# A recurrent scan's small products placed differently: output products behind the next chunk's solved rows, triangular products of eight chunks in one run

## The chip, the cores and the metric

The kernel runs on one core of a Trainium2 chip. Its five engines work side by side, each through its own list of instructions in order: TensorE (PE, matrix products into PSUM), VectorE (DVE), ScalarE (ACT), GpSimd (POOL) and SyncE (SP), which issues the transfers. The metric is the device time of one execution in microseconds; lower is better.

## What is computed

A decoder trunk of two layers on 1024 tokens of width 1024. Each layer normalizes its input, projects it (`h @ w_in`), runs three token mixers (pooling, retention, RWKV-7), gates and projects each, merges them and adds the result to the residual. The change concerns RWKV-7 alone, 8 heads of width 64:

```python
def step(S, inp):
    r_t, w_t, k_t, v_t, a_t, b_t = inp
    sa = jnp.einsum('bhvk,bhk->bhv', S, a_t)
    S = (S * w_t[:, :, None, :] + sa[..., None] * b_t[:, :, None, :]
         + v_t[..., None] * k_t[:, :, None, :])
    return S, jnp.einsum('bhvk,bhk->bhv', S, r_t)

_, y = lax.scan(step, jnp.zeros((B, H, N, N), jnp.float32), xs)
```

Everything else of the layer (`proj = h @ w_in`, the branch and output projections) is large matrix products.

## The kernel before

**Work.** The large products run as 128 x 128 weights against 128 x 512 moving columns; each value is split into a high and a low part, so that three products stand for one (`hhi`, `hlo` against `wh`, `wl`). The RWKV recurrence is computed in chunks of 64 tokens: 16 chunks for 1024 tokens, two heads at a time, so four head pairs (`hp`) in each of two layers make eight scans. `rwkv_task` is the generator for one head pair:

- `prepare(h)` makes, for each half `h` of eight chunks, the tiles `AR` (receptance and key side) and `BK` (key and value side).
- `scores(h)` transposes `BK` into `BKt`, then multiplies `BK` by `AR` for each chunk and head. The result is masked by VectorE into the triangular matrices `G`. Each head's operands stand on 64 partitions, so the products of two heads use 64 rows of the array each. This is done in two groups of four chunks, `q` = 0 and 1, each group written to two banks of PSUM, `gps`, and each followed by two masked multiplies.
- `invert`, `states` and `blocks` solve the triangular systems of all chunks ahead of the scan; `AV` holds what does not depend on the state.
- the scan then goes through the chunks `c` = 0 to 15. For each: the product `sa` of `AR` with the state `S` (into `cy`); VectorE adds `AV` and gives `xst`; two products per head pair give the solved rows (into `ch`), which ScalarE copies to `Z`; the state product `BKt` by `Z` gives the new state `Sn` on VectorE; and the output products `G` by `Z`, one for each head, are added in `cy` to what `sa` left there, and ScalarE copies them to `y`. After eight chunks `y` is normalized and handed to `rwkv_post`.

All of these are float32 products, and each appears in the profile as two instructions.

**PSUM.** There are eight banks: three for the large products (`acc`), two taken in turn by small work (`mx`), and three in the pool `psc`: the two halves of `two`, which `cyt()` gives out alternately, and `ch`.

**Order.** Nothing runs when it is written. Class `Log` records each operation with its operands; `plan()` lists all operations in an order for each engine by estimated durations, dependencies and a key (the place in the program plus `BIAS` of the lane; the lane `rwkv` goes 3000 places ahead); `emit()` then writes the instructions in this order, fixed at build time. Operations inside `with nc.together()` become one unit that stays in one run. An entry `o.after[p] = 2` says that `o` may be placed once `p` has started, without waiting for its end. While the operations are recorded, generators yield times in nanoseconds that decide when the next part is recorded among the large products. PE gets the large products wherever no operation of a lane with a lower key is ready.

**Exemption in the scan.** `sa` of chunk `c` writes one half of `two` while the copy of the output of chunk `c - 1` reads the other. `sa.no_dep` takes away that dependency, and `sa.own_dep` puts in the one on the copy of chunk `c - 2`, which reads the same half.

All instructions are recorded through one line of `emit()`, so that the profile shows line 550 for all, and its rows are told apart by the names of tiles: `ch<-xst,G` are the solved rows, `ch<-Z,BKt` the state product, `two<-Z,G` the output products, `two<-S,AR` the product `sa`, `g<-AR,BK` and `two<-AR,BK` the triangular products, `av<-Z,G` the products of `states`, and `acc<-...` the large products.

Of the kernel before, what the change touches and what calls it, by code (L numbers as in the profile page):

```python
# [9 lines left out]
F32 = mybir.dt.float32  # L10
# [3 lines left out]
ALU = mybir.AluOpType  # L14
# [3 lines left out]
P = 128  # L18
# [4 lines left out]
HF = 512  # L23
# [7 lines left out]
RWKV_EPS = 64e-5  # L31
# [532 lines left out]
def trunk_kernel(ctx, tc, xT, cvec, pos, vecs, consts, w_ada, w_all, pool_w, lora_w, out):  # L564
    nc = Log(tc.nc, tc)
# [15 lines left out]
    ps_c = pool("psc", 1, space=PSUM)  # L581
# [9 lines left out]
    def nm(s):  # L591
        uid[0] += 1
        return f"{s}_{uid[0]}"
# [9 lines left out]
    t_ri = slot("ri", 14)  # L603
# [7 lines left out]
    def mx(s):  # L611
        t = ps_m.tile([P, HF], F32, tag="mx", name=nm(s))
        if len(mxq) == 2:
            behind[t.name] = mxq.popleft()
        mxq.append(t.name)
        return t
# [4 lines left out]
    def cyt():  # L621
        turn[0] ^= 1
        return two[:, turn[0] * HF : (turn[0] + 1) * HF]
# [7 lines left out]
    o = CST["bone"]  # L631
    bone = cp.tile([P, P], F32R, name="bone")
    xst = cp.tile([P, P], F32, name="xst")
# [174 lines left out]
    hd = [dp.tile([8, 2, P, HF], F32, name=f"hd{l}") for l in range(L)]  # L808
# [11 lines left out]
    behind = {}  # L820
# [56 lines left out]
    def wait(*aps, spare=0.0):  # L877
        settle()
        names = [x.tensor.name if hasattr(x, "tensor") else x.name for x in aps]
        t = max(ready.get(n, 0.0) for n in names) + spare  # L880
        if len(mxq) == 2:
            t = max(t, ready.get(mxq[0], 0.0) + 600)
        return max(0.0, t - clock[0])
# [55 lines left out]
    def add(k, task):  # L939
        if not lanes[k]:  # L940
            due[k] = clock[0]
        lanes[k].append(task)
        return task

    def mmul(out, lhsT, rhs, start=True, stop=True, timed=False, **kw):
        n = rhs.free_size()
        fast = rhs.dtype == F32R
        settle()
        await_(out, *(() if timed else (lhsT, rhs)))
        m = lhsT.free_size()  # L950
        clock[0] += (n + 32) / 2.4 if fast else 2 * max(n, 1.6 * m - 92, m - 16) * 0.875
        return nc.tensor.matmul(out, lhsT=lhsT, rhs=rhs, start=start, stop=stop, **kw)
# [10 lines left out]
    posts = {}  # L963
# [236 lines left out]
    def layer_norm(y, n, w, eps, tile_, eng=nc.vector):  # L1200
        y3 = y.rearrange("p (n w) -> p n w", w=w)
        mean = sp.tile([P, n], F32, tag="mn", name=nm("mn"))
        nc.vector.tensor_reduce(mean, y3, axis=mybir.AxisListType.X, op=ALU.add)
        nc.vector.tensor_scalar_mul(mean, mean, 1.0 / w)
        yc = tile_("yc")
        yc3 = yc.rearrange("p (n w) -> p n w", w=w)
        eng.tensor_tensor(
            yc3, y3, mean.unsqueeze(2).to_broadcast([P, n, w]), op=ALU.subtract
        )
        sq = tile_("ysq")  # L1210
        nc.scalar.square(sq, yc)
        var = sp.tile([P, n], F32, tag="vr", name=nm("vr"))
        nc.vector.tensor_reduce(
            var, sq.rearrange("p (n w) -> p n w", w=w), axis=mybir.AxisListType.X, op=ALU.add
        )
        rsqrt(var, eps, 1.0 / w)
        eng.tensor_tensor(yc3, yc3, var.unsqueeze(2).to_broadcast([P, n, w]), op=ALU.mult)
        return yc
# [81 lines left out]
    def rwkv_task(l, hp, kT, rT, vp, lt):  # L1300
        lw = lora_load(l, hp)
        AR = r8("AR").rearrange("p (c j t) -> p c j t", j=2, t=CH)
        BK = r8("BK").rearrange("p (c j t) -> p c j t", j=2, t=CH)
        Gf = gtile("G")
        G = Gf[:, 0 : 32 * P].rearrange("p (u n) -> p u n", n=P)
# [3 lines left out]
        Z = r8("Z").rearrange("p (c n) -> p c n", n=P)  # L1309
        pc = sp.tile([P, 16], F32, tag="pc", name=nm("pc"))  # L1310
        c3 = lambda t: t.rearrange("p (c t) -> p c t", t=CH)
        rm = cs("rmask", P).unsqueeze(1).to_broadcast([P, 4, P])
        jt = lambda t, rows, c: t[rows, c, :, :].rearrange("p j t -> p (j t)")
        bvs, rks = [], []
# [91 lines left out]
        def scores(h):  # L1406
            yield max(until(whole[h] + 1000), wait(Z, spare=600))
            for q in range(2):
                ps = mx("bt")
                c0 = 8 * h + 4 * q  # L1410
                n = min(4, 15 - c0)
                with nc.together():
                    for c in range(n):
                        trans(ps[:, c * P : (c + 1) * P], jt(BK, slice(0, P), c0 + c), timed=True)
                nc.scalar.copy(BKt[:, c0 : c0 + n, :], ps[:, 0 : n * P].rearrange("p (c n) -> p c n", n=P))
                yield 1300
            for q in range(2):
                c0 = 8 * h + 4 * q
                gps = [mx("g"), cyt()]
                with nc.together():  # L1420
                    for j in range(4):
                        for hd in range(2):
                            rows = slice(64 * hd, 64 * hd + 64)
                            mmul(gps[hd][:, j * P : (j + 1) * P], jt(BK, rows, c0 + j), jt(AR, rows, c0 + j), timed=True)
                for hd in range(2):
                    u0 = 16 * hd + c0
                    nc.vector.tensor_tensor(
                        G[:, u0 : u0 + 4, :], gps[hd].rearrange("p (u n) -> p u n", n=P), rm, op=ALU.mult
                    )
                yield 2600  # L1430
            yield from bonus(h)
# [9 lines left out]
        start = [0.0]  # L1441
# [85 lines left out]
        for S in SS:  # L1527
            nc.gpsimd.memset(S, 0.0)
        yield wait(MT, *SS)
        yout = []  # L1530
        for c in range(16):
            par = c % 2
            prog[(l, hp)] = c
            if c % 8 == 0:
                y = t_ri("y")
            S, Sn = SS[par], SS[1 - par]
            cy = cyt()
            if c == 0:
                nc.scalar.copy(xst[0:64, :], AV[:, 0:P])
            else:  # L1540
                if c < 15:
                    SP = sb.tile([P, P], F32, tag="SP", name=nm("SP"), bufs=1)
                    nc.scalar.activation(SP, S, AF.Copy, scale=pc[:, c : c + 1])
                sa = mmul(cy[:, 0:P], jt(AR, slice(0, P), c), S)
                sa.no_dep = yout[-1]
                sa.after[yout[-1]] = 2
                if c > 1:
                    sa.own_dep = yout[-2]
                nc.vector.tensor_tensor(xst[0:64, :], cy[64:128, 0:P], AV[:, c * P : (c + 1) * P], op=ALU.add)
            yield wait(xst)  # L1550
            ch = ps_c.tile([P, HF], F32, tag="ch", name=nm("ch"))
            for hd in range(2):
                cols = slice(64 * hd, 64 * hd + 64)
                u0 = (16 * hd + c) * P
                n = 65
                mmul(ch[0:n, cols], Gf[:, u0 + 64 : u0 + 64 + n], xst[:, cols])
            nc.scalar.copy(Z[0:64, c, :], ch[0:64, 0:P])
            yield wait(Z)
            if c < 15:
                mmul(ch[:, P : 2 * P], BKt[:, c, :], Z[:, c, :])  # L1560
            for hd in range(2 if c < 15 else 0):
                rw = slice(64 * hd, 64 * hd + 64)
                new = ch[rw, P + 64 * hd : P + 64 * hd + 64]
                if c == 0:
                    nc.vector.tensor_scalar_mul(Sn[rw, rw], new, pc[rw, 0:1])
                else:
                    nc.vector.scalar_tensor_tensor(
                        Sn[rw, rw], new, pc[rw, c : c + 1], SP[rw, rw], op0=ALU.mult, op1=ALU.add
                    )
            yield 500  # L1570
            for hd in range(2):
                cols = slice(64 * hd, 64 * hd + 64)
                mmul(
                    cy[0:65, cols],
                    G[:, 16 * hd + c, 0:65],
                    Z[:, c, cols],
                    start=c == 0,
                    skip_group_check=True,
                )
            o = (c % 8) // 2 * P  # L1580
            yout.append(nc.scalar.copy(y[64 * par : 64 * par + 64, o : o + P], cy[0:64, 0:P]).ins)
            yield wait(Sn)
            if c % 8 == 7:
                h = c // 8
                yn = layer_norm(y, 8, 64, RWKV_EPS, t_ri, nc.gpsimd)
                posts[l, hp, h] = add("post", rwkv_post(l, hp, h, yn, bvs[h]))

    def rwkv_post(l, hp, h, yn, bv):
        yield 6500
        yield wait(yn, spare=3000)  # L1590
        ps = mx("yt")
        with nc.together():
            for j in range(4):
                trans(ps[:, j * P : (j + 1) * P], yn[:, j * P : (j + 1) * P])
        ob = t_ri("wob")
        nc.vector.scalar_tensor_tensor(ob, ps, vv(l, "ln_w", hp), bv, op0=ALU.mult, op1=ALU.add)
        store(od[l][2, hp, h], ob)
        yield 100
# [981 lines left out]
```

## Time and profile before

| | |
|---|---|
| three runs, median | 2252.29 us |
| three runs, lowest to highest | 2251.56 to 2252.78 us |
| the profiled run | 2251.25 us |
| its span, first to last instruction | 2249.4 us |
| mean granted clock of TensorE | 0.996 |

The page gives for each engine its busy time. In views by tile or in the timeline a row has the engine, the operation, `out<-in` by the names of tiles, the shapes (for a product: rows x columns of the weights, written 128*65, then the moving operand, 128x64) and a count. Durations of products overlap, since they are pipelined; the distance from one start to the next says what one takes of the engine. A bracket at the end of a row gives the engine's idle time before it and what ended that.

### The profile page before, as it was taken

Reading aid. Unit: us, or ns where it says so; the run is one execution under the profiler, and the core shown is the slowest. Engines: PE = TensorE matmul, PEld = TensorE weight load, DVE = VectorE, ACT = ScalarE, POOL = GpSimd, SP = SyncE. Lnnn points to the kernel's source line nnn. Section 1 sums busy time; section 2 is a strip of 40 time slices with the busy share of each in tenths; the row PEclk is TensorE's granted clock in tenths of the full one; section 3 lists DMA queues with packets and bytes.
Section 4 is the critical chain, followed back from the end, with each engine's and each line's share of the span. In section 5 each row is a group of like instructions: output and inputs, shape, how many; then the busy total and the mean of one; then the engine's idle time right before and its main releaser. Section 6 shows DMA issues by size and latency. Waiting matters only on the chain. (4 is left out here: it accounts for less than half of the span.)

```text
span 2249.4 us, 34694 instructions
## 1 busy us (share of the span) xinstructions
PE 2214.6 (98%) x12836; PEld 1847.6 (82%) x12836; DVE 1637.2 (73%) x2865; ACT 953.6 (42%) x1829; POOL 595.3 (26%) x538
## 2 busy tenths in 40 slices
PE   7999999999999999999999999999999999999998
PEld 6788888888888888888878888888888888888887
DVE  7996886967878765669787678577686844465895
ACT  5634434434344344324464353353443444451254
POOL 2223323333325233320042132333333500041100
PEclk9999999999999999999999999999999999999999
DMA  9222111112236663754440111111123533257343
GB/s 321 69 59 72 34 43 42 48 48 70 85 114 214 201 207 127 238 178 146 145 163 28 48 40 44 48 46 49 36 86 94 176 121 112 86 165 232 117 141 113
DMA packets 138041, 247.77 MB, mean 110 GB/s; under 512 B 15632, under 2 KB 19984, under 8 KB 137872
## 3 DMA queue, kind: packets, MB, share of 16 engines
q1 hardware_dynamic: 137872, 245.56, 34.0%
q8 instruction: 101, 1.65, 0.3%
q14 instruction: 68, 0.56, 0.1%
HBM read 185.99 MB, written 59.51 MB: 109 GB/s over the span
## 5 line engine op out<-in xcount | busy, mean ns | idle before, releaser
L550 PE MATMUL acc<-hhi,wh 128*128 128x512 f32 x1488 | 596.9, 401 | 1.6 <-DVE vp L550 1.1
L550 PE MATMUL acc<-hhi,wl 128*128 128x512 f32 x1488 | 596.8, 401 | 0.0
L550 PE MATMUL acc<-hlo,wh 128*128 128x512 f32 x1488 | 596.4, 401 | 0.0
L550 PEld LDWEIGHTS acc<-hhi,wh 128*128 128x128 f32 x1488 | 280.5, 189 | 50.7 <-DVE vp L550 1.5
L550 PEld LDWEIGHTS acc<-hhi,wl 128*128 128x128 f32 x1488 | 280.6, 189 | 48.6
L550 PEld LDWEIGHTS acc<-hlo,wh 128*128 128x128 f32 x1488 | 280.6, 189 | 47.4
L550 POOL TENSOR_TENSOR wl<-wr,wh 128x512 fp32r<-128x512 f32 x143 | 189.8, 1327 | 474.9 <-ACT wh L550 343.2
L550 ACT CAST wh<-wr 128x512 fp32r<-128x512 f32 x226 | 139.5, 617 | 251.1 <-PE acc L550 191.3
L550 PE MATMUL acc<-T,wh 128*128 128x512 f32 x576 | 177.5, 389 | 0.0
L550 DVE SCALAR_TENSOR_TENSOR S<-ch,pc,SP 64x64 f32<-64x64 f32 x224 | 63.3, 283 | 86.9 <-PE ch L550 84.1
L550 PEld LDWEIGHTS acc<-T,wh 128*128 128x128 f32 x576 | 108.1, 188 | 22.4
L550 ACT CAST wh<-wsum 128x512 fp32r<-128x512 f32 x112 | 69.5, 621 | 121.1 <-PE acc L550 117.3
L550 DVE TENSOR_TENSOR wl<-wsum,wh 128x512 fp32r<-128x512 f32 x79 | 56.2, 712 | 79.0 <-ACT wh L550 78.7
L550 PE MATMUL acc<-T,wl 128*128 128x512 f32 x288 | 112.1, 389 | 0.0
L550 ACT COPY Z<-ch 64x128 f32<-64x128 f32 x128 | 33.1, 259 | 132.3 <-PE ch L550 131.7
L550 DVE TENSOR_TENSOR wl<-wraw,wh 128x512 fp32r<-128x512 f32 x60 | 42.0, 699 | 63.2 <-ACT wh L550 63.2
L550 DVE TENSOR_TENSOR tm<-MT,two 64x30 f32<-64x30 f32 (+14 forms) x240 | 76.3, 318 | 11.4 <-ACT two L550 4.6
L550 POOL TENSOR_TENSOR oz<-ol,oz 128x512 fp32r<-128x512 f32 x10 | 14.1, 1405 | 264.6 <-DVE wl L550 179.7
L550 DVE TENSOR_TENSOR two<-two,tm 64x30 f32<-64x30 f32 (+14 forms) x240 | 78.9, 329 | 7.1
L550 ACT CAST wh<-wraw 128x512 fp32r<-128x512 f32 x84 | 52.0, 619 | 70.8 <-PE acc L550 50.1
L550 PE MATMUL acc<-oy,wh 128*128 128x512 f32 x256 | 80.0, 393 | 0.0
L550 PE MATMUL acc<-oG,wh 128*128 128x512 f32 x256 | 78.9, 389 | 0.0
(340 smaller groups left out, 4914.3 us busy)
## 6 DMA issues: line engine op xcount, KB each, us to landing
wr<-in_w_all SPq DMA_DIRECT2D x246, 256.0 KB, 2.7
wraw<-in_w_all SPq DMA_DIRECT2D x112, 256.0 KB, 2.9
gd<-gsg SPq DMA_DIRECT2D x96, 256.0 KB, 2.0
gs<-gd SPq DMA_DIRECT2D x96, 256.0 KB, 3.5
wada<-in_w_ada SPq DMA_DIRECT2D x80, 256.0 KB, 3.1
ol<-od SPq DMA_DIRECT2D x48, 256.0 KB, 3.6
traw<-hd SPq DMA_DIRECT2D x32, 256.0 KB, 2.9
x<-in_xT SPq DMA_DIRECT2D x16, 256.0 KB, 5.1
```

Source lines behind the costliest of these rows:

```text
L550: o.inst = f(*a, **k)
```

## The change

In `scores` the loop over `q` no longer makes products. One run under `together` makes those of all eight chunks of a half, into four banks: one of `mx`, the two halves of `two`, and `ch`. The masked multiplies stay in the loop.

In the scan the output products, their copy, and the end of a half move into a function `outputs(c, cy, behind)`. It is called for chunk `c - 1` in chunk `c`, after the products of the solved rows and the copy to `Z`, and both heads' products are one unit that may be placed as soon as the last product of the solved rows has started. Chunk 15 gets its own call behind the loop. The exemption of `sa` (`no_dep`, `own_dep`) and the pause of 500 before the outputs are gone.

```diff
+            gps = [mx("g"), cyt(), ps_c.tile([P, HF], F32, tag="ch", name=nm("ch")), cyt()]
+            with nc.together():
+                for j in range(8):
+                    for hd in range(2):
+                        rows = slice(64 * hd, 64 * hd + 64)
+                        o = j % 4 * P
+                        mmul(
+                            gps[j // 4 * 2 + hd][:, o : o + P], jt(BK, rows, 8 * h + j), jt(AR, rows, 8 * h + j), timed=True
+                        )
             for q in range(2):
-                c0 = 8 * h + 4 * q
-                gps = [mx("g"), cyt()]
-                with nc.together():
-                    for j in range(4):
-                        for hd in range(2):
-                            rows = slice(64 * hd, 64 * hd + 64)
-                            mmul(gps[hd][:, j * P : (j + 1) * P], jt(BK, rows, c0 + j), jt(AR, rows, c0 + j), timed=True)
                 for hd in range(2):
-                    u0 = 16 * hd + c0
+                    u0 = 16 * hd + 8 * h + 4 * q
                     nc.vector.tensor_tensor(
-                        G[:, u0 : u0 + 4, :], gps[hd].rearrange("p (u n) -> p u n", n=P), rm, op=ALU.mult
+                        G[:, u0 : u0 + 4, :], gps[2 * q + hd].rearrange("p (u n) -> p u n", n=P), rm, op=ALU.mult
                     )
                 yield 2600
...
-        yout = []
+        ys = [None, None]
+
+        def outputs(c, cy, behind=None):
+            if c % 8 == 0:
+                ys[c // 8] = t_ri("y")
+            y = ys[c // 8]
+            with nc.together():
+                for hd in range(2):
+                    cols = slice(64 * hd, 64 * hd + 64)
+                    o = mmul(
+                        cy[0:65, cols],
+                        G[:, 16 * hd + c, 0:65],
+                        Z[:, c, cols],
+                        start=c == 0,
+                        skip_group_check=True,
+                    )
+            if behind is not None:
+                o.after[behind] = 2
+            o = (c % 8) // 2 * P
+            r = slice(64 * (c % 2), 64 * (c % 2) + 64)
+            nc.scalar.copy(y[r, o : o + P], cy[0:64, 0:P])
+            if c % 8 == 7:
+                h = c // 8
+                yn = layer_norm(y, 8, 64, RWKV_EPS, t_ri, nc.gpsimd)
+                posts[l, hp, h] = add("post", rwkv_post(l, hp, h, yn, bvs[h]))
+
+        cy = None
         for c in range(16):
...
-            cy = cyt()
+            before, cy = cy, cyt()
...
-                sa = mmul(cy[:, 0:P], jt(AR, slice(0, P), c), S)
-                sa.no_dep = yout[-1]
-                sa.after[yout[-1]] = 2
-                if c > 1:
-                    sa.own_dep = yout[-2]
+                mmul(cy[:, 0:P], jt(AR, slice(0, P), c), S)
...
-                mmul(ch[0:n, cols], Gf[:, u0 + 64 : u0 + 64 + n], xst[:, cols])
+                last = mmul(ch[0:n, cols], Gf[:, u0 + 64 : u0 + 64 + n], xst[:, cols])
             nc.scalar.copy(Z[0:64, c, :], ch[0:64, 0:P])
+            if c:
+                outputs(c - 1, before, last)
             yield wait(Z)
...
-            yield 500
-            for hd in range(2):
-                cols = slice(64 * hd, 64 * hd + 64)
-                mmul(
-                    cy[0:65, cols],
-                    G[:, 16 * hd + c, 0:65],
-                    Z[:, c, cols],
-                    start=c == 0,
-                    skip_group_check=True,
-                )
-            o = (c % 8) // 2 * P
-            yout.append(nc.scalar.copy(y[64 * par : 64 * par + 64, o : o + P], cy[0:64, 0:P]).ins)
             yield wait(Sn)
-            if c % 8 == 7:
-                h = c // 8
-                yn = layer_norm(y, 8, 64, RWKV_EPS, t_ri, nc.gpsimd)
-                posts[l, hp, h] = add("post", rwkv_post(l, hp, h, yn, bvs[h]))
+        outputs(15, cy)
```

More of the change, by code (lines that the diff above doesn't have):

```diff
@@ L1533, in rwkv_task @@
             prog[(l, hp)] = c
-            if c % 8 == 0:
-                y = t_ri("y")
             S, Sn = SS[par], SS[1 - par]
-            cy = cyt()
+            before, cy = cy, cyt()
             if c == 0:
```

## The prediction

> **What bounds the kernel now.** I read first the head of the page and the busy time in two windows, then the timeline of TensorE (PE) around single small products, and last the rows of the tiles that the change touches. The head of the page, then the windows (columns: PE, weight loads, VectorE, ScalarE, GpSimd, clock, DMA):
>
> ```profile
> span 2249.4 us, 34694 instructions
> ## 1 busy us (share of the span) xinstructions
> PE 2214.6 (98%) x12836; PEld 1847.6 (82%) x12836; DVE 1637.2 (73%) x2865; ACT 953.6 (42%) x1829; POOL 595.3 (26%) x538
> ```
>
> ```profile
> 0.00:100.00 100.00, 82.01 (x356) 67.04 (x357) 83.65 (x151) 60.52 (x98) 27.83 (x39) 0.95 0.61 217
> 100.00:2249.40 2149.40, 2132.60 (x12482) 1780.55 (x12480) 1553.52 (x2715) 893.09 (x1733) 567.50 (x500) 1.00 0.33 105
> ```
>
> PE is busy for 98% of the span. It stands still for 18.0 us in the first 100 us, which the change does not touch, and for 2149.4 - 2132.6 = 16.8 us in all the rest, at full clock. So after the start there is almost nothing to win by shortening a wait of the scan, and nearly every nanosecond that a step takes away from PE's own stream comes off the time. The question is therefore not how long the chain of a chunk is, but how much PE time its small products take among the large ones. One chunk of the scan, on PE and then on ScalarE (start, duration, instruction):
>
> ```profile
> 187.37 0.40 PE L550 MATMUL acc<-hhi,wl 128*128 128x512 f32 x1
> 187.60 0.40 PE L550 MATMUL ch<-xst,G 128*65 128x64 f32 x4
> 187.81 0.48 PE L550 MATMUL acc<-hhi,wh 128*128 128x512 f32 x1
> 188.13 0.39 PE L550 MATMUL acc<-hlo,wh 128*128 128x512 f32 x1
> ...
> 188.59 0.39 PE L550 MATMUL acc<-hhi,wh 128*128 128x512 f32 x1
> 188.82 0.38 PE L550 MATMUL ch<-Z,BKt 128*128 128x128 f32 x2
> 189.04 0.40 PE L550 MATMUL two<-Z,G 128*65 128x64 f32 x4
> 189.25 0.48 PE L550 MATMUL acc<-hlo,wh 128*128 128x512 f32 x1
> 189.56 0.39 PE L550 MATMUL acc<-hhi,wl 128*128 128x512 f32 x1
> 189.79 0.40 PE L550 MATMUL acc<-hhi,wh 128*128 128x512 f32 x1
> 190.03 0.39 PE L550 MATMUL acc<-hlo,wh 128*128 128x512 f32 x1
> 190.25 0.38 PE L550 MATMUL two<-S,AR 128*128 128x128 f32 x2
> 190.39 0.48 PE L550 MATMUL acc<-hhi,wl 128*128 128x512 f32 x1
> 190.71 0.39 PE L550 MATMUL acc<-hhi,wh 128*128 128x512 f32 x1
> ```
>
> ```profile
> 188.04 0.26 ACT L550 COPY Z<-ch 64x128 f32<-64x128 f32 x1 [1.52 <-PE ch L550]
> 188.20 0.62 ACT L550 CAST wh<-wr 128x512 fp32r<-128x512 f32 x1
> 189.47 0.26 ACT L550 COPY y<-two 64x128 f32<-64x128 f32 x1 [0.65 <-PE two L550]
> ```
>
> Durations overlap, so I price a run of small products by starts. Large products alone follow each other every 0.23 us (189.56, 189.79, 190.03). The price of a run is the time from the large product before it to the second large product after it, less two such steps (0.46). The solved rows alone: 188.13 - 187.37 - 0.46 = **0.30 us**. State product and output products in one run: 189.56 - 188.59 - 0.46 = **0.51 us**. Within a run each instruction of 64 columns costs little, as a long run of the same shape (65 columns of weights, 64 moving) shows:
>
> ```profile
> 279.93 0.48 PE L550 MATMUL acc<-hlo,wh 128*128 128x512 f32 x1
> 280.25 3.00 PE L550 MATMUL av<-Z,G 128*65 128x64 f32 x48
> 283.06 0.48 PE L550 MATMUL acc<-hhi,wl 128*128 128x512 f32 x1
> 283.37 0.40 PE L550 MATMUL acc<-hhi,wh 128*128 128x512 f32 x1
> ```
>
> The 48 cost 283.37 - 279.93 - 0.46 = 2.98 us and the four above 0.30, so one costs (2.98 - 0.30) / 44 = 0.061 us, and a run has 0.30 - 4 x 0.061 = about 0.06 us that is paid once, by the switch from and to large products. That once-paid part is what both halves of the change save.
>
> **The change part by part.** *Outputs behind the solved rows.* Today a chunk pays two such runs with 64-column products: the solved rows, and state plus outputs. Afterwards the outputs of the chunk before stand in the run of the solved rows, and the state product stands alone. No product is added or removed. The new run is not in this trace. From the slope it costs 0.30 + 4 x 0.061 = 0.54 us. Its bounds are 0.51 (187.60 to 187.81 is 0.21 for four, added to 0.30) and 0.60 (two runs of 0.30 that share nothing); I take 0.54, since the 48-product row has the very same shape. The state product alone (two instructions, 128 x 128) is not in the trace either. The nearest row is the S product (two instructions of the same shape) at 190.25. It costs 190.71 - 190.03 - 0.46 = 0.22 us. A chunk then pays 0.54 + 0.22 = 0.76 instead of 0.30 + 0.51 = 0.81: **0.05 us less**, with bounds of 0.08 less and 0.01 more. This applies to 15 chunks in each of 8 scans, 120 in all. The row of the output products, with their first and last start:
>
> ```profile
> L550 PE MATMUL two<-Z,G x512: 217/222/223, 175.7 to 1766.5; 128*65 128x64 f32 x171
> ```
>
> I counted in the timeline between these two: some 103 of the 120 runs of state and outputs border on a large product; the others border on more small work, and there the switch was shared already, so I count nothing. 103 x 0.05 = **5.2 us**, bounds 8.2 gained and 1.0 lost.
>
> The output copy on ScalarE moves with its products; its 0.26 us is hidden as before, ScalarE being busy 42%. The cover is the room up to the S product of the next chunk, which must wait for that copy, since it writes the bank that is read (the exemption in the code goes). In the rows above Z's copy ends at 188.30, the output copy would end at about 188.56, and the next S product starts at 190.25: 1.7 us of room. If a cast of 0.62 us stands between, 1.1 us are left. Behind a late S product in PE's queue all large products would wait too. The output products themselves add no wait: Z of the chunk before has been read by the state product already. They stand ahead of the state product, but that waits for Z's copy, and large products fill that gap now (188.13 to 188.82), so four small ones take the place of one of them.
>
> *Triangular products.* They come as groups of 16 instructions on 64 rows, and there are (256 + 256) / 16 = 32 groups. The rows of the tile g, then a group alone, and two groups that the order has put in one run already:
>
> ```profile
> L550 PE MATMUL g<-AR,BK x256: 272/272/373, 102.4 to 1657.6; 64*128 64x128 f32 x128
> ```
>
> ```profile
> 102.11 0.40 PE L550 MATMUL acc<-hhi,wh 128*128 128x512 f32 x1
> 102.43 0.37 PE L550 MATMUL g<-AR,BK 64*128 64x128 f32 x1
> ...
> 103.53 0.50 PE L550 MATMUL nps<-ksh,bone 128*128 128x512 f32 x1
> 103.86 0.39 PE L550 MATMUL nps<-ksl,bone 128*128 128x512 f32 x1
> ```
>
> ```profile
> 417.62 0.40 PE L550 MATMUL acc<-hlo,wh 128*128 128x512 f32 x1
> 417.95 0.37 PE L550 MATMUL g<-AR,BK 64*128 64x128 f32 x1
> ...
> 419.94 0.50 PE L550 MATMUL acc<-hhi,wl 128*128 128x512 f32 x1
> 420.27 0.39 PE L550 MATMUL acc<-hhi,wh 128*128 128x512 f32 x1
> ```
>
> Alone a group costs 103.86 - 102.11 - 0.46 = 1.29 us; two in one run cost 420.27 - 417.62 - 0.46 = 2.19. Joining saves 2 x 1.29 - 2.19 = 0.39 us. I counted the groups in the timeline between the two ends of the row above: 14 of the 32 stand in 7 joined runs today and 18 stand alone. So only 9 joins are new, not 16: 9 x 0.39 = **3.5 us**. The masked multiplies on VectorE stay four of the same size for each half. The first two start some 0.9 us later, the last two no later, and with VectorE behind a PE that has other work this costs nothing; without that cover it is 0.9 us in each of 16 halves, 14 us. The wait for a third and a fourth bank is met: the scan before has read them long ago. That one shared buffer fewer is taken may save a wait; I count nothing.
>
> **The sum**: 5.2 + 3.5 = 8.7 us off the span of 2249.4, so 2240.7. The profiled run took 2251.25, 1.85 more than its span, and the median of the runs is 2252.29, 1.04 above that. 2252.3 - 8.7 = **2243.6 us**.
>
> **One rule weighed.** The Trainium skill, in "TensorE: Matmul & The Clock Gate", Part 2, says that the next weights are loaded while the running matmul streams, pulled ahead of it by the queue. By that rule the place of the outputs would not matter, the scan would win nothing, and the first rival below would come true. The rows speak against it for 64-column products, by the 0.06 us paid once for each run.
>
> The same skill, in "Perfetto Trace Analysis", section "Identifying the Most-Contended Engine", calls matmul busy time a poor measure and asks for the share of weight loads, which is 82% here; by that PE would have headroom and the change might win nothing (the last rival).
>
> **The rivals.**
> 1. *The outputs' place does not matter*, or the order made at build time puts large products between them and the solved rows. Then the scan pays 0.30 + 0.30 + 0.22 = 0.82, nothing is won there, and only the groups count: 2252.3 - 3.5 = 2248.8. For it: the two runs have the same once-paid 0.06 wherever they stand alone. Against: the code releases the outputs as soon as the last product of the solved rows has started.
> 2. *The new order eats the gain.* The order of all engines is planned anew, so other waits fall elsewhere. After the first 100 us there are 16.8 us of waits; if these grow by half (8.4), the time is about 2252. For it: any edit shifts the planner. Against: the large products always give PE something to do.
> 3. *The S product waits for the output copy*, the slower side. The room is 1.7 us. Two casts ahead of the copy put its end at 188.30 + 1.24 + 0.26 = 189.80, still in time; a third puts it at 190.42, 0.17 us late. From there on it decides: in 120 chunks 0.17 us each is 20 us, less the 8.7 won, so 2264. Against: one cast stands there in the rows, not three.
> 4. *PE is not what bounds*: then nothing moves, 2252.3. Against: the even steps of 0.23 us.
>
> **How the numbers follow.** Forecast 70%, rival 1 8%, rival 2 14% (a quarter of it beyond its 2252), rival 3 6%, rival 4 2%. The measurement can tell 0.2%, 4.5 us, so faster means under 2247.8, slower over 2256.8. Faster: 70%. Within: 8 + 11 + 2 = 21%. Slower: 3 + 6 = 9%. The unknown costs alone span 2252.3 - 8.2 - 3.5 = 2240.6 to 2252.3 + 1.0 - 3.5 = 2249.8. I widen this to 2238 (a few waits fewer by the new order) and to 2252 (rivals 1 and most of 2), which leaves out rivals 3 and the tail of 2.
>
> **What the profile afterwards would show.** Right: runs of solved rows and outputs of about 0.54 us, state products alone at 0.22, sixteen runs of 32 triangular instructions at about 2.2 us, PE's busy time 8 to 9 us lower and its idle time still about 35 us. Wrong: large products between solved rows and outputs (rival 1), the same savings beside more idle time of PE (rival 2), or idle time before the S product put down to ScalarE's copy of y (rival 3).

## The result and the profile after

The changed kernel took 2241.59 us (median of seven runs, 2237.41 to 2247.1) where the kernel before took 2252.29 (seven runs, 2251.11 to 2252.78). The ratio is 0.9954 [0.9941, 0.9967], a gain of 10.4 us [7.4, 13.3]. The forecast was 2243.6, a gain of 8.7. The profiled run took 2239.61 us.

The head of the page after, and the windows of the same two stretches (columns: PE, weight loads, VectorE, ScalarE, GpSimd, clock, share of DMA, GB/s):

```profile
span 2237.8 us, 34658 instructions
## 1 busy us (share of the span) xinstructions
PE 2206.3 (99%) x12836; PEld 1845.6 (82%) x12836; DVE 1646.9 (74%) x2864; ACT 953.1 (43%) x1829; POOL 607.0 (27%) x539
```

```profile
0.00:100.00 100.00, 84.25 (x350) 70.76 (x351) 81.88 (x149) 59.79 (x96) 26.66 (x39) 0.98 0.62 217
100.00:2237.80 2137.80, 2122.03 (x12488) 1774.83 (x12486) 1565.04 (x2716) 893.34 (x1734) 580.33 (x501) 1.00 0.34 106
```

PE does the same 12836 products in 2206.3 us instead of 2214.6, 8.3 us less. It stands still for 2237.8 - 2206.3 = 31.5 us, where it was 34.8; after the first 100 us that is 2137.80 - 2122.03 = 15.8, where it was 16.8. So most of the gain is work that became shorter, and little of it is a wait that went. The share of weight loads stayed at 82% while the time fell.

One chunk of the scan after the change, on PE and then on ScalarE (start, duration, instruction):

```profile
189.88 0.40 PE L550 MATMUL acc<-hlo,wh 128*128 128x512 f32 x1
190.11 0.40 PE L550 MATMUL ch<-xst,G 128*65 128x64 f32 x4
190.35 0.40 PE L550 MATMUL two<-Z,G 128*65 128x64 f32 x4
190.56 0.47 PE L550 MATMUL acc<-hhi,wl 128*128 128x512 f32 x1
190.87 0.39 PE L550 MATMUL acc<-hhi,wh 128*128 128x512 f32 x1
191.09 0.39 PE L550 MATMUL acc<-hlo,wh 128*128 128x512 f32 x1
191.33 0.38 PE L550 MATMUL ch<-Z,BKt 128*128 128x128 f32 x2
191.47 0.47 PE L550 MATMUL acc<-hhi,wl 128*128 128x512 f32 x1
191.78 0.39 PE L550 MATMUL acc<-hhi,wh 128*128 128x512 f32 x1
192.01 0.40 PE L550 MATMUL acc<-hlo,wh 128*128 128x512 f32 x1
192.24 0.40 PE L550 MATMUL acc<-hhi,wl 128*128 128x512 f32 x1
192.48 0.39 PE L550 MATMUL acc<-hhi,wh 128*128 128x512 f32 x1
192.70 0.39 PE L550 MATMUL acc<-hlo,wh 128*128 128x512 f32 x1
192.93 0.38 PE L550 MATMUL two<-S,AR 128*128 128x128 f32 x2
```

```profile
190.55 0.26 ACT L550 COPY Z<-ch 64x128 f32<-64x128 f32 x1 [1.19 <-PE ch L550]
190.83 0.26 ACT L550 COPY y<-two 64x128 f32<-64x128 f32 x1
```

Priced as in the prediction, the run of solved rows and outputs costs 190.87 - 189.88 - 0.46 = 0.53 us (estimated 0.54), and the state product alone 191.78 - 191.09 - 0.46 = 0.23 (estimated 0.22). The copy to `y` ends at 191.09, 1.84 us before the next S product. One thing differs that the prediction did not look for: between the state product and the S product there are now six large products, where there were four and the outputs.

A run of 32 triangular instructions after the change, again on PE:

```profile
399.54 0.40 PE L550 MATMUL acc<-hlo,wh 128*128 128x512 f32 x1
399.86 0.37 PE L550 MATMUL g<-AR,BK 64*128 64x128 f32 x1
...
401.85 0.50 PE L550 MATMUL nps<-ksh,bone 128*128 128x512 f32 x1
402.18 0.39 PE L550 MATMUL nps<-ksl,bone 128*128 128x512 f32 x1
```

It costs 402.18 - 399.54 - 0.46 = 2.18 us; the prediction had 2.19.

### The profile page after: what moved, and what is told of

Its sections match the earlier page's. It is cut to its first block, busy times and chain, and to the rows that moved or that the text cites. A ratio compares the mean times of both kernels' runs of the same rounds, so it can differ in the third digit from the quotient of the medians.

```text
span 2237.8 us, 34658 instructions
## 1 busy us (share of the span) xinstructions
PE 2206.3 (99%) x12836; PEld 1845.6 (82%) x12836; DVE 1646.9 (74%) x2864; ACT 953.1 (43%) x1829; POOL 607.0 (27%) x539
## 5 line engine op out<-in xcount | busy, mean ns | idle before, releaser
L550 POOL TENSOR_TENSOR wl<-wr,wh 128x512 fp32r<-128x512 f32 x145 | 198.0, 1366 | 446.4 <-ACT wh L550 340.8
L550 ACT ACTIVATE SP<-S,pc 128x128 f32<-128x128 f32 x112 | 45.0, 402 | 112.6 <-DVE S L550 112.1
```

What stands on the lines that cost most here:

```text
L550: o.inst = f(*a, **k)
```

## The experiments

Beside the ratio to the kernel before, I give for each run a number from its trace that separates PE's own work from waits. For every product I took the time to the next start. Over all fourteen traces, the 10th percentile of this time for the same sequence of five shapes (the product, two before it and two after) is the price of the product there. The sum of the prices, from the first to the last product, I call the **stream**: what this kernel's order of products costs PE when nothing is late and the clock is full. What is left of the time between these two products is the **rest**: waits, stretches at lower clock and jitter. The stream is a derived number, not one that the profiler measures, and it depends on the choice made: with three shapes instead of five, or the 25th percentile or the median instead of the 10th, the change comes out at 8 to 11 us under the kernel before, `groups_only` at 3 to 5 and `outputs_only` at 5 to 7. Its differences hold to about a microsecond. Each ratio is to runs of the kernel before that were taken beside that kernel's; their medians lay between 2251.87 and 2252.52 us.

| kernel | ratio [95%] | median us | stream us | rest us |
|---|---|---|---|---|
| before | | 2252.29 | 2129.4 | 106.5 |
| the change | 0.9954 [0.9941, 0.9967] | 2241.59 | 2119.3 | 105.0 |
| groups_only | 0.9971 [0.9961, 0.9982] | 2246.07 | 2125.3 | 105.4 |
| outputs_only | 1.0028 [1.0018, 1.0038] | 2257.75 | 2123.4 | 117.1 |
| outputs_apart | 0.9967 [0.9955, 0.998] | 2244.28 | 2124.8 | 106.7 |
| after_again | 0.9957 [0.9944, 0.9969] | 2241.9 | 2119.3 | 109.4 |
| before_order1 | 0.9986 [0.9977, 0.9996] | 2248.96 | 2129.3 | 103.9 |
| before_order2 | 1.0003 [0.9994, 1.0013] | 2253.74 | 2129.4 | 111.1 |
| outputs_order1 | 0.9998 [0.9989, 1.0008] | 2251.95 | 2124.2 | 112.1 |
| outputs_order2 | 1.0035 [1.0022, 1.0049] | 2260.14 | 2124.0 | 120.8 |
| outputs_tight | 0.9965 [0.9951, 0.9978] | 2244.38 | 2124.1 | 105.3 |
| after_tight | 0.994 [0.9928, 0.9953] | 2239.27 | 2119.7 | 101.4 |
| after_order1 | 0.9947 [0.9935, 0.996] | 2240.32 | 2119.0 | 106.1 |
| after_order2 | 0.9924 [0.9912, 0.9936] | 2234.39 | 2118.9 | 101.5 |

### Each half alone

`groups_only` is the kernel before with only the edit of `scores`. `outputs_only` is the change with the old loop of `scores`:

```diff
-            gps = [mx("g"), cyt(), ps_c.tile([P, HF], F32, tag="ch", name=nm("ch")), cyt()]
-            with nc.together():
-                for j in range(8):
...
             for q in range(2):
+                c0 = 8 * h + 4 * q
+                gps = [mx("g"), cyt()]
+                with nc.together():
+                    for j in range(4):
```

> The kernel before with the triangular products of eight chunks in one run, the outputs where they were. Theory (PE time once paid per run): 16 runs of these products instead of 25, 9 x 0.39 = 3.5 us less, a ratio of 0.9984; the profile has PE 3 to 4 us less busy and as much idle. Rival (the new order of everything else made the gain): no fixed share, any ratio between 0.995 and 1.002, with the difference in idle time or in runs that hold no triangular product.

> The kernel before with only the output products moved behind the solved rows of the next chunk; triangular products in groups of four chunks. Theory: a run of solved rows and outputs at 0.53 us and a state product alone at 0.23 instead of 0.30 and 0.51, some 0.05 us for each of about 104 chunks whose runs border on large products, 5 us less, a ratio of 0.9978. Rival (the freed chain of the scan, not PE's own time): scans shorter by several us each and a ratio as low as 0.996, or no gain at all if it was luck of the order.

The groups alone gain 0.29% [0.18, 0.39], about 6.5 us; their stream is 4.1 us shorter. The ratio is below the 0.9984 expected, and the sign expected in the profile, PE 3 to 4 us less busy and as much idle, is met only after the first 100 us, where PE is busy for 2129.32 us instead of 2132.60 and idle for 15.3 instead of 16.8; over the whole span PE is only 0.9 us less busy (2213.7). The two profiles differ in the first 100 us, where the granted clock is 0.98 instead of 0.95. The outputs alone make the kernel **slower** by 0.28% [0.18, 0.38], about 6 us, although their stream is 6.0 us shorter than before; the 0.9978 expected was missed. So PE's work became cheaper as forecast, and the rest grew by 117.1 - 106.5 = 10.6 us. The waits of PE in `outputs_only` (engine, tile, what it waited for: us in total, times, longest) have two that the kernel before does not have:

```profile
PE acc L550 <- ACT wh L550: 2.7, 1, 2.7
PE two L550 <- DVE G L550: 2.7, 1, 2.7
```

The windows around these two places show what followed them (same columns as above):

```profile
607.00:613.00 6.00, 2.83 (x96) 2.30 (x96) 5.89 (x5) 0.58 (x1) 0.28 (x1) 1.00 0.00 0
613.00:620.00 7.00, 7.00 (x61) 5.47 (x54) 3.81 (x6) 1.99 (x4) 3.53 (x3) 0.51 0.25 77
685.00:710.00 25.00, 21.70 (x90) 17.07 (x89) 19.89 (x25) 13.29 (x25) 18.39 (x13) 0.93 0.58 190
```

And PE's timeline at the second place:

```profile
695.49 0.48 PE L550 MATMUL acc<-hhi,wl 128*128 128x512 f32 x1
698.70 0.80 PE L550 MATMUL acc<-hhi,wh 128*128 128x512 f32 x1 [2.73 <-ACT wh L550]
699.29 0.63 PE L550 MATMUL acc<-hlo,wh 128*128 128x512 f32 x1
699.72 0.63 PE L550 MATMUL acc<-T,wh 128*128 128x512 f32 x1
```

In the first window PE is busy for 2.83 of 6 us while VectorE is busy for 5.89: PE has run out of large products and has only the small ones of a scan's preparation left, which wait for VectorE. At 698.70, behind the last scan of the layer, it waits for a cast of weights, which had itself waited 1.40 us for their transfer. After either wait the granted clock is half: 0.51 in the second window, and large products start 0.59 and 0.43 us apart where 0.23 is their step at full clock. The records of the clock show half clock for 6.8 us from 613.1 and for 3.4 us from 698.5. The two waits and half of the two slow stretches are 2.7 + 2.7 + 10.2 / 2 = 10.5 us, about the growth of the rest.

### Is it the luck of one order?

The planner makes a new order for any edit. To see how much that alone moves, I let it shake its keys, outside the scan's lane, by up to 20 places either way, with two seeds, for the kernel before, the outputs alone and the whole change:

```diff
-SEED = 0
-SHAKE = 0
+SEED = 1
+SHAKE = 40
```

(`SEED = 2` in the kernels ending in order2.)

> The kernel before, same work, with the planner's keys outside the scan's lane shifted at random by up to 20 places (seed 1), so that the other engines' and the large products' order differs. Theory A (PE's stream is what it was, only waits move): PE's busy time within 2 us of before, the ratio anywhere from 0.998 to 1.005 by the waits that this order has. Theory B (the order hardly matters): 1.000 within 0.001.

> As before_order1 with seed 2. A: another ratio from 0.998 to 1.005, by its waits. B: 1.000 within 0.001.

> The outputs alone moved, as in outputs_only, with the same shift of keys (seed 1). Theory A: the saving of 5 us in PE's stream is there in any order, and what made outputs_only 6 us slower were two waits of 2.7 us of its order and the half clock after each; where this order has no wait over 2 us in the scans, the ratio is about 0.9975, and 5 us less than before_order1 if that has none either. Theory C (moving the outputs costs time by itself): again about 1.003.

> As outputs_order1 with seed 2. A: about 0.9975 without a wait over 2 us in the scans, up to 1.003 with two of them. C: about 1.003.

> The whole change with the planner's keys outside the scan's lane shifted by up to 20 places (seed 1), as in before_order1. Theory A: PE's stream 10 us less than in the orders of before; the waits are this order's own; 0.995 without a wait over 2 us in the scans, 0.998 with two. If the gain of the change was luck of one order: 0.999 or more.

> As after_order1 with seed 2: 0.995 to 0.998, by its waits, against 0.999 or more if the gain was luck.

Order alone moves the kernel before by 0.14% down and 0.03% up, and the outputs alone between 0.9998 and 1.0035. The whole change is at 0.9947 and 0.9924, under every order of the kernel before; the second is also under the 0.995 to 0.998 expected. PE's busy time did not stay within 2 us of the kernel before, as theory A had it: in `before_order2` it is 2222.3 us, 7.7 more. Its stream is that of the kernel before; busy time also counts what makes products last longer, such as half clock (0.63 to 0.80 us for a large product in the rows above, where 0.39 is usual), and is no good measure of PE's work here. The streams hardly move: 2129.3 to 2129.4 before, 2123.4 to 2124.2 with the outputs, 2118.9 to 2119.3 with both. Only the rest moves. So the savings on PE belong to the change and not to an order, and the outputs alone give them back in three orders of three. Both shaken kernels of `outputs_only` show waits of 1.8 to 2.1 us near 613 or 693 to 700 us, each followed by half clock. The kernel before can have one such place too: `before_order2` waits 2.87 us near 1177, with 3.4 us at half clock behind it. The kernel before waits 1.47 us at the same place and keeps its clock, so this accounts for 2.87 - 1.47 + 3.4 / 2 = 3.1 of the 4.6 us by which the rest of `before_order2` is larger.

### Why PE runs dry with the outputs alone

My theory was that the scan had become longer. The planner allows 300 ns (`MARGIN`) for the way from another engine to a product, and fills the time with whole large products. Taken from the starts of all chunks, the median time from the state product to the next S product is 1.44 us before (outputs and four large products between) and 1.61 in `outputs_only` and in the change (six large). The mean time from one chunk's solved rows to the next goes from 4.19 us to 4.35 in `outputs_only` and 4.33 in the change. A longer scan takes up more large products, and by my theory these are missing later, where a scan is being prepared. The rival was that the outputs' place itself, or the missing exemption, makes the waits. The experiment gives the S product a smaller allowance and leaves the rest of the program, though the planner makes its order anew:

```diff
-                    gap += MARGIN
+                    gap += 150 if u.ins_[-1].tensor.name.startswith("S_") else MARGIN
```

> The outputs alone moved, as in outputs_only, and the planner's allowance for the S product cut from 300 to 150, so that five large products stand between the state product and the S product instead of six. Same work. Theory D (the move takes 5 us from PE's stream but makes the chain of a chunk 0.17 us longer, since six large products replace four large and the outputs; eight scans come 2 to 4 us later each, PE runs out of other work in layer 0 and waits, and its clock halves): scans back at 60 to 65 us each, no wait over 1.5 us and no half clock between 100 and 2200 us, PE's stream 5 us shorter; ratio 0.9975. Theory C (the move or its order costs time whatever the chain is): 1.003 as in outputs_only, with waits at the same places.

> The changed kernel with the same cut of the allowance. Theory D: scans 2 to 3 us shorter each, PE's stream as in the changed kernel, the wait and half clock near 1782 us gone, 0.9945 to 0.9955, a little below the changed kernel. Theory C: as the changed kernel or slower by waits of the new order.

In `outputs_tight` five large products stand between, and the S product starts 194.95 - 193.58 = 1.37 us after the state product:

```profile
193.58 0.38 PE L550 MATMUL ch<-Z,BKt 128*128 128x128 f32 x2
193.72 0.48 PE L550 MATMUL acc<-hhi,wh 128*128 128x512 f32 x1
...
194.95 0.27 PE L550 MATMUL two<-S,AR 128*128 128x128 f32 x1
```

The same windows as for `outputs_only`:

```profile
607.00:613.00 6.00, 6.00 (x43) 5.07 (x42) 5.20 (x11) 2.65 (x7) 2.58 (x2) 1.00 0.16 40
613.00:620.00 7.00, 6.88 (x42) 5.49 (x41) 2.83 (x8) 1.94 (x5) 2.58 (x2) 1.00 0.12 43
685.00:710.00 25.00, 25.00 (x112) 20.68 (x111) 23.47 (x25) 12.01 (x21) 13.23 (x9) 1.00 0.69 231
```

PE is full where it stood still, the clock is 1.00, and the time is 0.9965 [0.9951, 0.9978] of the kernel before, some 13 us under `outputs_only` (2244.38 against 2257.75). The stream is still 5.3 us shorter than before. One number in the planner turns the outputs alone from a loss into a gain, with the outputs in the same place and the exemption gone as before, so neither of these two makes the loss by itself, and an edit that shortens the scans removes it. That the longer scans caused it is not shown. From its first to its last solved rows a scan takes 62.8 us in the mean before, 65.3 in `outputs_only` and 64.9 in the change, but 60.6 in `outputs_tight`, so that the experiment did not go back to the old length but well below it. And `outputs_apart`, shown further down, has the longest scans of all, 66.7 us, with a rest of only 106.7. On the whole change the same edit gives 0.994 [0.9928, 0.9953], which is not told apart from the change itself.

What the traces do not settle is why the whole change is free of these waits with chunks as long. The three scans ahead of the first wait take 199.0 us together in `outputs_only` and 199.1 in the change, which does not wait there (196.8 before). Nor does it help to look at how early the scans begin. In layer 0 the four distances from the first transpose into `BKt` to the first solved rows sum to 277.6 us before, 279.3 in `outputs_only` and 266.6 in the change, which would fit; but they sum to 276.5 in `outputs_tight`, which has no such wait, and to 265.8 in `outputs_order1`, which has one. It stays open.

### Does the place behind the solved rows matter?

This is the prediction's first rival. `outputs_apart` is the whole change, but the outputs may be placed only once the copy to `Z` has started, so that a large product comes between:

```diff
-                last = mmul(ch[0:n, cols], Gf[:, u0 + 64 : u0 + 64 + n], xst[:, cols])
-            nc.scalar.copy(Z[0:64, c, :], ch[0:64, 0:P])
+                mmul(ch[0:n, cols], Gf[:, u0 + 64 : u0 + 64 + n], xst[:, cols])
+            last = nc.scalar.copy(Z[0:64, c, :], ch[0:64, 0:P])
```

> The changed kernel, but the outputs may be placed only once the copy to Z has started, so that one large product or more comes between the solved rows and the outputs, and both are runs of their own. Same products, same chunk, same copies. Theory: solved rows 0.30, outputs 0.30, state product 0.23 a chunk, 0.83 against 0.76 in the changed kernel and 0.81 before; the scan's gain is gone, about 0.06 x 104 = 6 us more than the changed kernel, only the triangular products' 3.5 us are left against before, 0.998. Rival (delay of the outputs by a chunk, the dropped exemption or the new order made the gain): as fast as the changed kernel, 0.9954.

PE in one chunk of it:

```profile
192.12 0.39 PE L550 MATMUL acc<-hhi,wl 128*128 128x512 f32 x1
192.34 0.40 PE L550 MATMUL ch<-xst,G 128*65 128x64 f32 x4
192.55 0.48 PE L550 MATMUL acc<-hhi,wh 128*128 128x512 f32 x1
192.87 0.40 PE L550 MATMUL two<-Z,G 128*65 128x64 f32 x4
193.07 0.47 PE L550 MATMUL acc<-hlo,wh 128*128 128x512 f32 x1
193.38 0.39 PE L550 MATMUL acc<-hhi,wl 128*128 128x512 f32 x1
```

The step back to large products is paid twice: 192.55 to 192.87 and 193.07 to 193.38 are 0.32 and 0.31 us, where a large product otherwise takes 0.23. The two runs cost 193.38 - 192.12 - 3 x 0.23 = 0.57 us where the joined one cost 0.53 (the starts are rounded to 0.01). The stream is 2124.8, 5.5 us above the change and 0.5 from `groups_only`: with a large product between, the scan's saving is gone. The time, 0.9967 [0.9955, 0.998], agrees with `groups_only`, but its interval overlaps that of the change, and its median is only 2.4 us above that of `after_again` (2244.28 against 2241.9), where 6 us were expected. So the stream and the rows tell them apart, and the time alone does not.

### The same kernel again

The first seven runs of the changed kernel spread over ten microseconds, those of the kernel before over less than two. `after_again` is the changed kernel with no edit.

> The changed kernel once more, beside the others on the same chip. Both theories: 0.9954 within its interval. Its single runs spread over 10 us before, where the kernel before spread over 1.7; if the spread comes from PE's clock or the first 100 us, a second profile differs from the first there and nowhere else.

It gave 0.9957 [0.9944, 0.9969] and, in its profiled run, a rest 4.4 us larger, with the same stream. PE waits 2.19 us for the low part of a weight tile, and 6.8 us of half clock follow. The cause in the timeline of GpSimd and PE, first in `after_again`:

```profile
1776.30 7.02 POOL L550 TENSOR_TENSOR tlo<-traw,thi 128x512 fp32r<-128x512 f32 x1 [4.36 <-ACT thi L550]
```

```profile
1784.59 0.80 PE L550 MATMUL acc<-hhi,wl 128*128 128x512 f32 x1 [2.19 <-POOL wl L550]
```

and then the same instruction in the first profile of the change:

```profile
1777.43 2.23 POOL L550 TENSOR_TENSOR tlo<-traw,thi 128x512 fp32r<-128x512 f32 x1 [4.35 <-ACT thi L550]
```

One GpSimd subtraction took 7.02 us in one execution and 2.23 in another of the same program, and GpSimd's next result came late. VectorE ran operations of the same size without a pause from before the 7.02 us began until 1782.19, and the subtraction ended 1.13 us after that; in the first profile three such operations of VectorE, at 1780.73, 1783.03 and 1784.73, took 1.77 us instead of 0.68 beside GpSimd's. So it looks as if the two engines hold each other up, but no run tests it. The wait and half the slow stretch are 2.19 + 3.4 = 5.6 us, about the difference of the rest; between 1783 and 1787 us the starts of the same products drift apart by 5.0 us. Whether this place accounts for the whole spread of the runs can't be seen, since only two of them were profiled.

## Why the prediction was right

- **PE's own stream is the bound.** Right for the whole change. The stream shrank by 10.1 us and the time by 10.4 [7.4, 13.3]. The rival that PE is not the bound is refuted. By the share of weight loads, the measure that the Trainium skill names in "Perfetto Trace Analysis", section "Identifying the Most-Contended Engine", PE would have had headroom; that share stood at 82% before and after while the time fell, and the measurement decides.
- **Outputs, 5.2 us.** Right for the stream, which fell by 5.2 to 6.0 us in the four kernels with this part alone. The time of three of these four did not fall with it, as a step further down says. The parts were sized well too: 0.53 and 0.23 us for 0.54 and 0.22.
- **Triangular products, 3.5 us.** Right within what the stream can tell: 4.1 us. The nine new joins were counted rightly, since the program's order has 25 triangular runs before and 16 after, so one join saves 4.1 / 9 = 0.46 us by this stream and 0.39 by the prediction; the microsecond of doubt in the stream covers the difference. The time of `groups_only` fell by 6.5 us [4.1, 8.8]; 1.1 us of that is the rest in its profile, which the prediction counted at nothing.
- **Room for the output copy, 1.7 us.** Right. Over all chunks of the changed kernel the copy to `y` ends 1.89 us (median) and never less than 1.49 before the next S product. Rival 3 did not come about.
- **The outputs take the place of a large product** between solved rows and state product. Right: that distance is 1.21 us in the median before and after, with four large products before and three after.
- **"The question is therefore not how long the chain of a chunk is."** This is the step that failed, without harm to the number. The outputs left the stretch between state product and S product, and the planner put two more large products there, which makes that stretch 0.17 us longer. With the outputs alone, waits and half clock then cost 10.5 us, more than the outputs won, and shorter scans removed them. Rival 2, a new order that eats the gain, was therefore real for this half, and "the large products always give PE something to do" was the wrong argument against it. That its 8.4 us, half of the 16.8 us of waits after the first 100 us, came near the 10.6 measured is chance: 8.7 of the 16.8 lie in the last 25 us of the span, behind all scans.
- **The sum, 8.7 us.** It came out, but in part by luck. The streams of the two halves add up, 4.1 + 6.0 = 10.1 us; their times do not, with 6.5 us gained and 6 lost against 10.4 gained together. In the whole change the waits of the outputs alone stayed away, in three orders of three. The prediction gave no ground for that, and no run explains it.
- **Rival 1**, that the place does not matter, is refuted by the stream and the rows of `outputs_apart`; its time alone does not decide. What the Trainium skill states in "TensorE: Matmul & The Clock Gate", Part 2, that the next weights are pulled ahead of a running product, does not make a run of 64-column products free: the return to large products costs 0.31 us instead of 0.23 each time.

The fastest kernel of the study was `after_order2`, 0.9924 [0.9912, 0.9936], under the change's interval. It is faster than both kernels by an order found by chance: its rest is 3.5 us smaller than that of the change, its stream the same within 0.4.

## What to carry to other kernels

Where the matrix engine is full, price small products by the distance of starts, once for each run and once for each instruction, and join runs that pay the same switch; the sum of such prices came out within 1.4 us here. Before taking work out of a stretch of a dependent chain, ask what the fixed order will put in its place: here it was two large products, which lengthened the chain, and with the outputs alone a shorter chain turned a loss into a gain. A wait of 2 us on the matrix engine may cost twice that, through the clock that follows it, so look at the granted clock behind each wait and not only at the wait.

## What the hardware showed

- Half clock followed waits that were shorter than I had thought needed. In these traces, between the first 100 us and the last 25, stretches of 3.4, 6.8 or 10.2 us at half clock followed waits of 2.66 and 2.73 us (`outputs_only`), 2.19 (`after_again`), and even 1.25 (`outputs_apart`, 3.4 us). In the 3.4 us ahead of each such stretch PE was busy for 0.9 to 2.0 us. The lengths are multiples of 3.4 us. The Trainium skill, "TensorE: Matmul & The Clock Gate", Part 1, has a free-running window of about 3.4 us, which agrees with the lengths; the rule that it gives there, no idle gaps over about 3.4 us, differs from these rows, where shorter waits sufficed. Not each wait of that size is followed by half clock. In `outputs_order2` PE waits 2.26 us near 1184 us, and the clock stays full; the line of its list of waits, and the window around:

```profile
PE acc L550 <- DVE r L550: 2.3, 1, 2.3
```

```profile
710.00:1775.00 1065.00, 1059.85 (x6178) 882.26 (x6177) 781.35 (x1366) 437.95 (x848) 283.40 (x252) 1.00 0.34 109
```

- A GpSimd subtraction of 128 x 512 took 2.23 us and 7.02 us in two executions of one program, the second while VectorE ran without a pause.
